# A transformer block on one core: gates ahead of the merges, operands made on demand, and a head that starts in 128-row pieces

## The chip, the cores and the metric

The kernel runs on one core of one Trainium2 chip. The metric is the device time of one execution, in microseconds (us). The core has five engines that run their own instruction streams: TensorE (PE, matrix products and transposes; PEld is its weight load), VectorE (DVE), ScalarE (ACT), GpSimd (POOL) and SyncE (SP). DMA transfers are issued from the queues of SP and ACT. They all run on the core's 16 DMA engines.

## The reference

One block of a hybrid network, in fp32, on x of 256 rows and 2048 columns (`T` = 256, `D` = 2048):

```python
h = rmsnorm(x, norm_ffn1);  x = x + 0.5 * (silu(h @ w1) * (h @ w3)) @ w2          # D_FF = 5632
h = rmsnorm(x, norm_mix)
(mq, mk, mv, mo, mi, mf, hq, hf, hi, hg, gate_m, gate_h) = split(h @ w_in)
y_m = mlstm_mixer(mq, mk, mv, mo, mi, mf, ...)       # 4 heads: conv, silu, gated attention, head norm
y_h = hgrn2_mixer(hq, hf, hi, hg, lb, ...)           # 8 heads: gated linear recurrence, head norm
merged = sigmoid(gate_m) * (y_m @ w_proj_m) + sigmoid(gate_h) * (y_h @ w_proj_h)
x = x + merged @ w_out
x = x + cross_attention(rmsnorm(x, norm_xattn), rmsnorm(mem, norm_mem), wq, wkv, wo)
h = rmsnorm(x, norm_ffn2);  x = x + 0.5 * (silu(h @ w1) * (h @ w3)) @ w2
return rmsnorm(x, norm_final)
```

All weights together are some 476 MB, and each is read once.

## The kernel before

**Products.** Every large product goes through `gemm_nat`. It makes a result of 256 x 512 (two PSUM banks from the pool `acc`, which has four) from 16 blocks of 128 rows of the weights, fewer for the projections. fp32 accuracy comes from a split: each operand is the sum of a high part rounded to fp32r and a low part, and three products are made per block: high by high (line 248), high by low weight (249), low operand by high weight (250). With two halves of the rows that is 6 products per block of 128 rows, 96 per full result of 2048 rows.

**Weights.** A `Unit` is a tile of 4 x 128 weight rows by 512 columns (1024 KB), loaded on SP's queue into one of four raw tiles (`wr`). A `Sub` is half of it: two blocks. `split` makes the high part (`wh`) with a cast on ACT and the low part (`wl`) with a subtraction on DVE, 1024 elements per partition each. `run` goes through the list of steps: before each Sub it loads units up to 7 Subs ahead, splits up to 3 ahead, then writes the 12 products and calls `tick`.

**Operands.** The left operand of a product is a pair of tiles (`oh`, `ol`) of 128 x 4 x 256, high and low, already transposed. A pair is turned either on PE (`turn`: four transposes of 128x128 per half, then cast and subtraction out of PSUM) or on DVE (`turn_on_vector`: 16 transposes of 32-row strips, `tt`, over four ticks, then cast and subtraction). These pairs and most other intermediate tiles come from one pool, `s4`, with 22 tiles.

**The planner.** Work beside the products is held in two lists. `timed` holds functions with the tick from which they are due (`after`). `bg` is a first-in, first-out list of background pieces: the HGRN and mLSTM mixers and the preparation of mem. `Paced` (line 90 is its call) adds up a planned cost per DVE and ACT instruction, a base plus a price per element. `tick` lets pieces go only while the planned backlog is under 2 us behind PE's planned time. `written` makes sure that a pair has been written before it is used, by running timed pieces; `flush` runs everything that is outstanding. Within each engine the instructions are put in order by the framework's scheduler, which may move an instruction ahead of an earlier one that has to wait.

**The mixer's end.** After the mLSTM values, for each of four column blocks c the kernel made the two gate products (gm, gh: 96 products each, from the norm's operands), then the projections of y_h (`evac_h`) and y_m (`evac_m`, which also adds and starts to turn the merged block). After the gates of c = 0 stood a flush, since the projections need `Y["h"]` and `Y["m"]`, which the background pieces make. Then four products with w_out follow.

**The head.** `setup` loads the identity, the first gains and, later, the other constants (705 KB) and small vectors on ACT's queue. `first` issues x in four chunks and the first weight units on SP's queue (`load_x`), turns x chunk 0 on PE, and puts the turns of the other chunks and the squares of the norm on ticks 1 to 7. The norm's factor is applied after the product, so the products wait only for x and the gains.

Of the kernel before, what the change touches and what calls it, by code (L numbers as in the profile page):

```python
# [19 lines left out]
P = 128  # L20
# [79 lines left out]
class Core:  # L100
    def __init__(self, nc):
        self.tensor, self.gpsimd, self.sync = nc.tensor, nc.gpsimd, nc.sync
        self.vector, self.scalar = Paced(nc.vector, 0.13, 0.00106), Paced(nc.scalar, 0.22, 0.00082)


class Block:
# [71 lines left out]
    def next_timed(self):  # L178
        i = min(range(len(self.timed)), key=lambda i: self.timed[i][0])
        self.timed.pop(i)[1]()  # L180

    def flush(self):
        while self.timed or self.bg:
            if self.timed:
                self.next_timed()
            else:
                self.bg.popleft()()

# [35 lines left out]

    def gemm_nat(self, ops, wap, n0, n, evac, kts=None, row0=0, late=0):

# [5 lines left out]
        def mm_for(k0, nk):  # L234
            def mm(hi, lo, ts=(0, 1)):
                if k0 == 0:
                    box["ps"] = [self.pacc([P, n]) for _ in range(2)]
                if k0 >= nkt - 2 * late and len(ts) == 2:
                    ts = (0,)
                    box.setdefault("late", []).append(lambda: mm(hi, lo, (1,)))  # L240
                for j in range(nk):
                    kt = k0 + j
                    xh, xl = self.written(pairs[kt // 4])
                    for t in ts:
                        sl = slice(t * P, (t + 1) * P)
                        a_h, a_l = xh[:, kt % 4, sl], xl[:, kt % 4, sl]
                        o = box["ps"][t]
                        nc.tensor.matmul(o, a_h, hi[:, j, :], start=(kt == 0), stop=False)  # L248
                        nc.tensor.matmul(o, a_h, lo[:, j, :], start=False, stop=False)  # L249
                        nc.tensor.matmul(o, a_l, hi[:, j, :], start=False, stop=(kt == nkt - 1))  # L250
# [16 lines left out]

    def turn(self, src, gain, dst, halves=(0, 1)):

        nc = self.nc  # L270
        hi, lo = dst
        for h in halves:
            ps = self.ps([P, 2, T])
            for j in range(2):
                for t in range(2):
                    c = (2 * h + j) * P
                    nc.tensor.transpose(ps[:, j, t * P:(t + 1) * P], src(t)[:, c:c + P], self.ident)  # L277
            if gain is None:
                nc.scalar.copy(hi[:, 2 * h:2 * h + 2, :], ps)
                nc.vector.tensor_sub(lo[:, 2 * h:2 * h + 2, :], ps, hi[:, 2 * h:2 * h + 2, :].bitcast(F32))  # L280
            else:
                for j in range(2):
                    k = 2 * h + j
                    g = gain[:, k:k + 1]
                    nc.scalar.activation(hi[:, k, :], ps[:, j, :], AF.Copy, scale=g)
                    nc.vector.scalar_tensor_tensor(
                        lo[:, k, :], in0=ps[:, j, :], scalar=g, in1=hi[:, k, :].bitcast(F32),
                        op0=ALU.mult, op1=ALU.subtract)
            if h == 1:
                self.unwritten.pop(id(dst), None)  # L290

    def pair(self):
# [3 lines left out]

    def written(self, p):

        while id(p) in self.unwritten:
            self.next_timed()  # L300
        return p

# [43 lines left out]
    def setup(self):  # L346
# [20 lines left out]

        def load(group):
            st = self.const.tile([P, P], F32, name=self.nm("stage"))
            first = group[0][1]  # L370
            for name, o, n in group:
                src = a[name]
                dims = " ".join("abc"[:len(src.shape)])
                src = src.rearrange(f"{dims} -> ({dims})")
                nc.scalar.dma_start(st[o - first:o - first + n, :], src.rearrange("(k p) -> k p", p=P))
            end = group[-1][1] + group[-1][2]
# [6 lines left out]
            return turn  # L383

        nc.scalar.dma_start(self.ident, a["consts"][:, :P])
        turn_first = load(groups[0])
        nc.vector.memset(self.mhalf, -0.5)

        def rest():
            nc.scalar.dma_start(c[:, P:], a["consts"][:, P:])  # L390
            turns = [load(g) for g in groups[1:]]
            self.gbias = self.const.tile([P, 8], F32, name="gbias")
            nc.scalar.dma_start(self.gbias[:, 0:4], a["mlstm_ig_bias"][0].partition_broadcast(P))
            nc.scalar.dma_start(self.gbias[:, 4:8], a["mlstm_fg_bias"][0].partition_broadcast(P))

# [6 lines left out]
        self.after(12, rest)  # L402
        return turn_first

    def lower_bounds(self):
# [36 lines left out]
    def rstd_of(self, ss, n, dim):  # L442
# [7 lines left out]
    def squares(self, src, ss_col):  # L450
        junk = self.t2([P, 512], name="junk")
        self.nc.scalar.activation(junk[:, :src.shape[-1]], src, AF.Square, accum_out=ss_col)

# [20 lines left out]

    def squares_of(self, n, c):
        for t in range(2):
            self.squares(self.x[c][:, t, :], n.ss[:, t, c:c + 1])
        n.count += 1
# [16 lines left out]
    def ffn(self, norm, w1, w3, w2, chunk_done, end=False):  # L495
        nc = self.nc
        ops = LazyOps(lambda: norm().ops)
        for f0, f1 in ((0, 6), (6, 11)):
            us = [None] * (f1 - f0)
            for f in range(f0, f1):  # L500
# [15 lines left out]

                self.gemm_nat(ops, w1, f * 512, 512, evac_a)
                self.gemm_nat(ops, w3, f * 512, 512, evac_b)
# [11 lines left out]
    def mixer(self, norm, chunk_done):  # L530
# [82 lines left out]

        merged = [None] * 4
        G = {}
        for c in range(4):
            for key, base in (("gm", 7176), ("gh", 9224)):
                def evac_g(ps, key=key):
                    r = norm().rstd
                    G[key] = self.t4([P, 2, 512], name=key)  # L620
                    for t in range(2):
                        nc.scalar.activation(G[key][:, t, :], ps[t], AF.Sigmoid, scale=r[:, t:t + 1])
                self.gemm_nat(ops, w, base + 512 * c, 512, evac_g)
            if c == 0:
                self.do(lambda: self.flush())

            def evac_h(ps):
                for t in range(2):
                    nc.vector.tensor_mul(G["gh"][:, t, :], ps[t], G["gh"][:, t, :])

            def evac_m(ps, c=c):
                gm, gh = G["gm"], G["gh"]
                for t in range(2):
# [15 lines left out]
    def hgrn_levels(self, h, b):  # L649
# [149 lines left out]
    def mlstm_weights(self, m):  # L799
# [17 lines left out]
        def head(h):  # L817
# [258 lines left out]
    def build(self):  # L1076
# [9 lines left out]

        def first(turn_gains):
            self.load_x()
            n = begin("norm_ffn1")
            n.ops = [self.pair() for _ in range(4)]  # L1090
            src = lambda c: (lambda t: self.x[c][:, t, :])
            turn_gains()
            for i in range(8):
                c, h = i // 2, i % 2
                fn = lambda c=c, h=h: self.turn(src(c), n.gain[:, 4 * c:4 * c + 4], n.ops[c], (h,))
                if i < 2:
                    fn()
                else:
# [78 lines left out]
```

## Time and profile before

| | |
|---|---|
| median of 3 runs | 2555.0 us (2554.29 to 2555.2) |
| the profiled execution | 2555.04 us |
| its span, first to last instruction | 2553.2 us |
| granted TensorE clock, mean | 0.998 |
| ACT table loads | 34, 43.6 us |
| DMA | 479.92 MB, mean 188 GB/s |

Times in the views are microseconds from the start of the span. A row of the timeline is start, duration, engine, line, operation, output <- input, count, and in brackets the idle time of the engine before it and what ended it. A row of waits is: who waited, for whom, us in total, times, longest. A row of windows gives the stretch, its length, busy time and number of instructions of PE, PEld, DVE, ACT and POOL, then granted clock, DMA share and GB/s. A row of groups gives count, busy us, mean ns, and the idle time before them. Products overlap in PE, so the length of one in a row (0.39) is more than the distance from one to the next.

### The profile page before, as it was taken

The page shows a single profiled execution, that of the slowest core. Times are in us where ns is not written, and L with a number is a line of the kernel's source. Part 1 is how long each engine was busy: PE and PEld are TensorE (multiplying, and loading weights), DVE is VectorE, ACT ScalarE, POOL GpSimd, SP SyncE. Part 2 cuts the span into 40 slices and gives each one's busy share as a digit, 9 for nine tenths or more (in the row PEclk, how much of TensorE's full clock was granted, in tenths as well). Part 3 has the DMA queues.
Part 4 walks back from the last instruction along what each step waited for, and adds up shares of the span by engine and source line. Part 5 has one row for each costly group of instructions (what it writes and reads, how often), then busy time and mean ns, then how long its engine had stood idle before and what let it go on. Part 6 is the DMA issues. An engine that isn't in the chain of part 4 may idle for free.

```text
span 2553.2 us, 29044 instructions
## 1 busy us (share of the span) xinstructions
PE 2528.8 (99%) x11431; PEld 2104.7 (82%) x11431; DVE 1730.7 (68%) x2384; ACT 1201.8 (47%) x1385; POOL 13.5 (1%) x21
## 2 busy tenths in 40 slices
PE   8999999999999999999999999999999999999998
PEld 7888888888888898787888888888888888888887
DVE  5767644767768878967666787677767574457664
ACT  5444434444455565644444454444544443344443
POOL 0000000000000000000000000000000000000000
PEclk9999999999999999999999999999999999999999
DMA  7665565565555545545555565555566556555653
GB/s 262 197 193 189 195 198 190 189 198 190 193 190 185 176 138 165 183 163 181 190 191 197 187 212 180 170 175 173 190 198 190 191 196 197 188 192 194 214 189 128
DMA packets 243305, 479.92 MB, mean 188 GB/s; under 512 B 8008, under 2 KB 14432, under 8 KB 243168
## 3 DMA queue, kind: packets, MB, share of 16 engines
q1 hardware_dynamic: 242016, 476.15, 57.4%
q10 hardware_dynamic: 1152, 1.92, 0.2%
q8 instruction: 89, 1.46, 0.2%
q14 instruction: 48, 0.39, 0.0%
HBM read 475.94 MB, written 2.10 MB: 187 GB/s over the span
## 4 chain that ended last, share of the span: by engine, by line
PE 92%; DVE 6%; issue 1%; ACT 0%; DMA 0%; POOL 0%; SPq 0%; POOLq 0%; ACTq 0%
PE pa L250 30%; PE pa L248 30%; PE pa L249 30%; DVE wl L90 2%; DVE tt L90 2%; PE ps L726 1%; DVE ol L90 1%; DVE cv L90 0%; PE ps L277 0%; DMA x<-in_x 0%; PE ps L966 0%; PE ps L967 0%; PE ps L965 0%; POOL rstd L447 0%; ACT kn L90 0%
## 5 line engine op out<-in xcount | busy, mean ns | idle before, releaser
L90 DVE TENSOR_TENSOR wl<-wr,wh 128x1024 fp32r<-128x1024 f32 (+1 forms) x904 | 1094.2, 1213 | 721.6 <-ACT wh L90 715.0
L90 ACT CAST wh<-wr 128x1024 fp32r<-128x1024 f32 (+1 forms) x904 | 942.0, 1045 | 1141.9 <-PE pa L250 1091.3
L248 PE MATMUL pa<-wh,oh 128*128 128x512 f32 (+1 forms) x3616 | 1409.7, 390 | 7.0 <-ACT oh L90 4.4
L249 PE MATMUL pa<-wl,oh 128*128 128x512 f32 (+1 forms) x3616 | 1403.6, 388 | 2.3 <-DVE wl L90 2.3
L250 PE MATMUL pa<-wh,ol 128*128 128x512 f32 (+1 forms) x3616 | 1402.5, 388 | 0.2 <-DVE ol L90 0.2
L248 PEld LDWEIGHTS pa<-wh,oh 128*128 128x128 f32 x3616 | 680.0, 188 | 143.3 <-ACT oh L90 4.8
L249 PEld LDWEIGHTS pa<-wl,oh 128*128 128x128 f32 x3616 | 680.2, 188 | 141.1 <-DVE wl L90 5.5
L250 PEld LDWEIGHTS pa<-wh,ol 128*128 128x128 f32 x3616 | 679.7, 188 | 138.8 <-DVE ol L90 0.7
L90 DVE STREAM_TRANSPOSE tt<-sil 32x256 f32<-32x256 f32 x352 | 153.6, 436 | 6.8
L90 DVE STREAM_TRANSPOSE tt<-x 32x256 f32<-32x256 f32 x144 | 62.8, 436 | 2.8
L90 ACT CAST oh<-tt 128x1024 fp32r<-128x1024 f32 x29 | 30.6, 1054 | 39.7 <-DVE tt L90 39.7
L90 ACT ACT_TABLE_LOAD x34 | 43.6, 1283 | 10.1 <-DVE rs L90 3.1
L90 ACT ACTIVATE oh<-tt,cols 128x256 fp32r<-128x256 f32 x52 | 23.3, 500 | 47.7 <-DVE tt L90 47.7
L90 ACT ACTIVATE sil<-pa,rstd 128x512 f32<-128x512 f32 x44 | 29.8, 689 | 17.8 <-PE pa L250 17.7
L90 DVE TENSOR_TENSOR ol<-tt,oh 128x1024 fp32r<-128x1024 f32 x29 | 35.4, 1220 | 1.6 <-ACT oh L90 1.4
L90 DVE STREAM_TRANSPOSE tt<-kn 32x256 f32<-32x256 f32 x64 | 27.9, 436 | 5.6 <-ACT kn L90 4.5
L90 DVE SCALAR_TENSOR_TENSOR sil<-pa,rstd,sil 128x512 f32<-128x512 f32 x44 | 31.0, 743 | 0.0
L90 DVE STREAM_TRANSPOSE qt<-qn 32x256 f32<-32x256 f32 x64 | 27.9, 436 | 4.1 <-ACT qn L90 3.0
L90 ACT ACTIVATE oh<-ps,cols 128x256 fp32r<-128x256 f32 x44 | 20.3, 473 | 21.4 <-DVE ol L90 15.6
L90 DVE COPY_PREDICATED at<-cst,ps 128x128 f32<-128x128 int32 x80 | 22.8, 328 | 10.6 <-PE ps L726 10.0
L90 ACT ACTIVATE junk<-x 128x512 f32<-128x512 f32 x40 | 24.9, 625 | 7.6 <-DVE x L90 7.0
L90 DVE SCALAR_TENSOR_TENSOR ol<-ps,cols,oh 128x256 fp32r<-128x256 f32 x44 | 20.7, 480 | 10.8 <-ACT oh L90 10.5
(174 smaller groups left out, 649.4 us busy)
## 6 DMA issues: line engine op xcount, KB each, us to landing
wr<-in_ffn_w SPq DMA_DIRECT2D x263, 1024.0 KB, 5.2
wr<-in_w_in SPq DMA_DIRECT2D x80, 1024.0 KB, 5.1
wr<-in_xattn_wkv SPq DMA_DIRECT2D x32, 1024.0 KB, 5.4
wr<-in_w_out SPq DMA_DIRECT2D x16, 1024.0 KB, 5.1
wr<-in_xattn_wq SPq DMA_DIRECT2D x16, 1024.0 KB, 5.0
wr<-in_xattn_wo SPq DMA_DIRECT2D x16, 1024.0 KB, 5.1
wr<-in_w_in SPq DMA_DIRECT2D x12, 688.0 KB, 4.1
wr<-in_w_proj_h SPq DMA_DIRECT2D x8, 1024.0 KB, 5.0
```

Source lines behind the costliest of these rows:

```text
L90: return fn(out, *args, **kw)
L248: nc.tensor.matmul(o, a_h, hi[:, j, :], start=(kt == 0), stop=False)
L249: nc.tensor.matmul(o, a_h, lo[:, j, :], start=False, stop=False)
L250: nc.tensor.matmul(o, a_l, hi[:, j, :], start=False, stop=(kt == nkt - 1))
L726: nc.tensor.matmul(ps[:, i, :], kt[:, g, j * P:(j + 1) * P], S["qc"][:, 2 * g + j, :], start=True, stop=True)
```

## The change

Six things are changed.

1. **Planner costs.** DVE from 0.13 + 0.00106 per element to 0.19 + 0.00104, ACT from 0.22 + 0.00082 to 0.25 + 0.00085; each `rstd_of` adds 0.9 to DVE's planned end.
2. **Operands on demand.** `written` takes the list and the index, and runs timed and background pieces until the operand exists and is written. The flush in the mixer is gone.
3. **Gates first.** The gates of c = 0, 1, 2 come before merge(0), the gates of c = 3 after it, then merges 1 to 3.
4. **From DVE to ACT.** `prep_f` of HGRN, and `di` and the copies into r0 and r1 of the mLSTM weights.
5. **The head.** Products of zeros (`warm`), 9 before x is turned and 4 behind the first piece; the first unit's Subs are four of one block each (`fine`); x chunk 0 is turned in four pieces of 128 columns, each followed by the split of its Sub; other turns and squares get other ticks; a first activation on the zeros.
6. **Order and queues.** The turns, the squares and the splits of the first 8 ticks are kept in program order on their engines. The constants and small vectors that are loaded at tick 12 are issued on SP's queue instead of ACT's.

```diff
-        self.vector, self.scalar = Paced(nc.vector, 0.13, 0.00106), Paced(nc.scalar, 0.22, 0.00082)
+        self.vector, self.scalar = Paced(nc.vector, 0.19, 0.00104), Paced(nc.scalar, 0.25, 0.00085)
...
+    def next_piece(self):
+        if self.timed:
+            self.next_timed()
+        else:
+            self.bg.popleft()()
...
-        self.nc.scalar.copy(s.hi, raw)
-        self.nc.vector.tensor_sub(s.lo, raw, s.hi.bitcast(F32))
+        pin = self.tc.keep_in_program_order if self.now < 8 else lambda ins: ins
+        pin(self.nc.scalar.copy(s.hi, raw))
+        pin(self.nc.vector.tensor_sub(s.lo, raw, s.hi.bitcast(F32)))
...
-                    xh, xl = self.written(pairs[kt // 4])
+                    xh, xl = self.written(pairs, kt // 4)
...
-            u = Unit(wap, row0 + k0 * P, 4, n0, n, 2)
-            for q in range(2):
-                self.steps.append(Sub(u, q, mm_for(k0 + 2 * q, 2)))
+            ns = 4 if fine and k0 == 0 else 2
+            u = Unit(wap, row0 + k0 * P, 4, n0, n, ns)
+            for q in range(ns):
+                self.steps.append(Sub(u, q, mm_for(k0 + 4 // ns * q, 4 // ns)))
...
+    def turn_piece(self, src, gain, dst, k, pin):
+        nc = self.nc
+        hi, lo = dst
+        ps = self.ps([P, T])
+        for t in range(2):
+            pin(nc.tensor.transpose(ps[:, t * P:(t + 1) * P], src(t)[:, k * P:(k + 1) * P], self.ident))
+        g = gain[:, k:k + 1]
+        pin(nc.scalar.activation(hi[:, k, :], ps, AF.Copy, scale=g))
+        pin(nc.vector.scalar_tensor_tensor(lo[:, k, :], in0=ps, scalar=g, in1=hi[:, k, :].bitcast(F32),
+                                           op0=ALU.mult, op1=ALU.subtract))
+        if k == 3:
+            self.unwritten.pop(id(dst), None)
...
-    def written(self, p):
-        while id(p) in self.unwritten:
-            self.next_timed()
-        return p
+    def written(self, ops, i):
+        while ops[i] is None or id(ops[i]) in self.unwritten:
+            self.next_piece()
+        return ops[i]
...
+        self.warm_tile = self.t2([P, P], name="warm")
+        nc.vector.memset(self.warm_tile, 0.0)
         nc.scalar.dma_start(self.ident, a["consts"][:, :P])
-        turn_first = load(groups[0])
+        turn_first = load(groups[0], nc.scalar)
+        self.tc.keep_in_program_order(
+            nc.scalar.activation(self.t2([P, 8], name="first"), self.warm_tile[:, 0:8], AF.Square))
...
-            nc.scalar.dma_start(c[:, P:], a["consts"][:, P:])
-            turns = [load(g) for g in groups[1:]]
+            nc.sync.dma_start(c[:, P:], a["consts"][:, P:])
+            turns = [load(g, nc.sync) for g in groups[1:]]
...
+    def warm(self, n):
+        ps = self.ps([P, P])
+        for _ in range(n):
+            self.nc.tensor.matmul(ps, self.warm_tile, self.warm_tile, start=True, stop=True)
...
         nc.gpsimd.tensor_tensor(r, ms, self.mhalf[:, :n], op=ALU.pow)
+        nc.vector.end += 0.9
...
-            if c == 0:
-                self.do(lambda: self.flush())
...
+        for c in range(3):
+            gates(c)
+        merge(0)
+        gates(3)
+        for c in range(1, 4):
+            merge(c)
...
-                nc.vector.tensor_scalar(f[:, i, :], f[:, i, :], self.oml[:, hd:hd + 1], self.lb[:, hd:hd + 1],
-                                        op0=ALU.mult, op1=ALU.add)
+                nc.scalar.activation(f[:, i, :], f[:, i, :], AF.Identity, scale=self.oml[:, hd:hd + 1],
+                                     bias=self.lb[:, hd:hd + 1])
...
-                nc.vector.tensor_scalar(di, self.ident, ig[t], None, op0=ALU.mult)
+                nc.scalar.activation(di, self.ident, AF.Copy, scale=ig[t])
...
-            nc.vector.tensor_copy(r0[:, 128:129], lf[0])
-            nc.vector.tensor_copy(r1[:, 0:129], lf[1].broadcast_to([P, 129]))
+            nc.scalar.copy(r0[:, 128:129], lf[0])
+            nc.scalar.copy(r1[:, 0:129], lf[1].broadcast_to([P, 129]))
...
         def first(turn_gains):
+            self.warm(9)
             self.load_x()
             n = begin("norm_ffn1")
             n.ops = [self.pair() for _ in range(4)]
             src = lambda c: (lambda t: self.x[c][:, t, :])
+            pin = self.tc.keep_in_program_order
             turn_gains()
-            for i in range(8):
+            first_subs = [st for st in self.steps if isinstance(st, Sub)][:4]
+            for k in range(4):
+                self.turn_piece(src(0), n.gain, n.ops[0], k, pin)
+                if k == 0:
+                    self.warm(4)
+                self.split(first_subs[k])
+            for i in range(2, 8):
                 c, h = i // 2, i % 2
-                fn = lambda c=c, h=h: self.turn(src(c), n.gain[:, 4 * c:4 * c + 4], n.ops[c], (h,))
-                if i < 2:
-                    fn()
-                else:
-                    self.after(i - 1, fn)
+                fn = lambda c=c, h=h: self.turn(src(c), n.gain[:, 4 * c:4 * c + 4], n.ops[c], (h,), pin)
+                self.after((1, 2, 4, 5, 6, 7)[i - 2], fn)
             for c in range(4):
-                self.after(4 + c, lambda c=c: self.squares_of(n, c))
+                self.after((5, 6, 8, 9)[c], lambda c=c: self.squares_of(n, c, pin=pin))
```

More of the change, by code (lines that the diff above doesn't have):

```diff
@@ L223, in run, with gemm_nat @@
         self.flush()
-    def gemm_nat(self, ops, wap, n0, n, evac, kts=None, row0=0, late=0):
+    def gemm_nat(self, ops, wap, n0, n, evac, kts=None, row0=0, late=0, fine=False):
         nc = self.nc
@@ L266, in gemm_nat, with turn @@
         self.do(finish)
-    def turn(self, src, gain, dst, halves=(0, 1)):
+    def turn(self, src, gain, dst, halves=(0, 1), pin=lambda ins: ins):
         nc = self.nc
@@ L366, in setup, with load @@
         self.stages = []
-        def load(group):
+        def load(group, engine):
             st = self.const.tile([P, P], F32, name=self.nm("stage"))
@@ L374, in load @@
                 src = src.rearrange(f"{dims} -> ({dims})")
-                nc.scalar.dma_start(st[o - first:o - first + n, :], src.rearrange("(k p) -> k p", p=P))
+                engine.dma_start(st[o - first:o - first + n, :], src.rearrange("(k p) -> k p", p=P))
             end = group[-1][1] + group[-1][2]
@@ L515, in evac_b @@
                     self.turn_on_vector(s, None, us[f - f0])
-                self.gemm_nat(ops, w1, f * 512, 512, evac_a)
+                self.gemm_nat(ops, w1, f * 512, 512, evac_a, fine=f == 0 and not end)
                 self.gemm_nat(ops, w3, f * 512, 512, evac_b)
@@ L611, in mixer, with gates @@
         self.do(lambda: self.bg.extend(self.mlstm_out(M, MV, MO)))
-        merged = [None] * 4
-        G = {}
-        for c in range(4):
+        merged, G = [None] * 4, {}
+        def gates(c):
             for key, base in (("gm", 7176), ("gh", 9224)):
@@ L619, in evac_g, with merge, evac_m @@
                     r = norm().rstd
[L620 removed]
+                    g = G[key, c] = self.t4([P, 2, 512], name=key)
                     for t in range(2):
[L622 removed]
+                        nc.scalar.activation(g[:, t, :], ps[t], AF.Sigmoid, scale=r[:, t:t + 1])
                 self.gemm_nat(ops, w, base + 512 * c, 512, evac_g)
[L624 to L625 removed]
+        def merge(c):
             def evac_h(ps):
                 for t in range(2):
[L629 to L632 removed]
+                    nc.vector.tensor_mul(G["gh", c][:, t, :], ps[t], G["gh", c][:, t, :])
+            def evac_m(ps):
+                gm, gh = G["gm", c], G["gh", c]
                 for t in range(2):
```

25 lines of the change are left out of this document (11 added, 14 removed).

## The prediction

> **What bounds the kernel now.** I read the page first: busy shares, then the chain that ended last.
>
> ```profile
> PE 2528.8 (99%) x11431; PEld 2104.7 (82%) x11431; DVE 1730.7 (68%) x2384; ACT 1201.8 (47%) x1385; POOL 13.5 (1%) x21
> PE 92%; DVE 6%; issue 1%; ACT 0%; DMA 0%; POOL 0%; SPq 0%; POOLq 0%; ACTq 0%
> ```
>
> TensorE (PE) is busy for 2528.8 of 2553.2 us, so 24.4 us of idle time is nearly all there is to win, unless products run slower than they could. The second view lists PE's waits.
>
> ```profile
> PE ps L381 <- DMA stage<-in_norm_ffn: 4.8, 1, 4.8
> PE pa L248 <- ACT oh L90: 4.4, 1, 4.4
> PE pa L248 <- ACT wh L90: 2.6, 1, 2.6
> PE pa L249 <- DVE wl L90: 2.3, 5, 0.5
> ```
>
> Four places: two at the start, one long wait for an operand (oh), and five short waits for the low part of a weight split. The third view counts PE's instructions (the x behind PE busy) by stretch; the row of 200 to 250 us is the steady state.
>
> ```profile
> 10.00:19.53 9.53, 9.11 (x32) 6.89 (x33) 5.88 (x7) 6.54 (x14) 0.00 (x0) 1.00 1.05 386
> 200.00:250.00 50.00, 50.00 (x222) 41.42 (x221) 35.15 (x45) 22.23 (x23) 0.00 (x0) 1.00 0.58 190
> 1020.00:1030.00 10.00, 8.50 (x36) 6.37 (x36) 9.65 (x19) 3.26 (x4) 0.00 (x0) 1.00 0.43 136
> 1030.00:1040.00 10.00, 9.22 (x39) 6.94 (x38) 9.82 (x20) 5.62 (x9) 0.00 (x0) 1.00 0.52 181
> 1040.00:1050.00 10.00, 10.00 (x44) 7.98 (x43) 9.71 (x18) 4.21 (x4) 0.00 (x0) 1.00 0.66 210
> 1147.89:1159.70 11.81, 7.15 (x16) 4.79 (x16) 11.30 (x19) 3.48 (x6) 0.00 (x0) 0.71 0.16 46
> ```
>
> Steady state is 50/222 = 0.225 us per product. Three stretches fall short. 1147.89 to 1159.70 holds 16 products, worth 3.6 us, in 11.81: **8.2 us lost**, of which only 4.4 are the wait. 1020 to 1040 holds 75 where 88 fit: 13 x 0.225 = **2.9 us lost**, with VectorE (DVE) busy 9.65 and 9.82 of 10. And 10.00 to 19.53 holds 24 products and 8 transposes. The chain gives four transposes at full pace:
>
> ```profile
> 15.31 0.43 PE pa L248
> ...
> 18.89 0.23 PE pa L249
> 19.12 0.23 PE pa L250
> 19.35 0.44 PE ps L277 x4
> ```
>
> So that stretch is worth 24 x 0.225 + 8 x 0.11 = 6.3 us and takes 9.53: **3.2 us lost**, because products there start every 0.43 us until about 16.1 and every 0.23 after that.
>
> **The change, part by part.**
>
> *Gates first (mixer).* The timeline around the loss:
>
> ```profile
> 1129.75 1.37 ACT L90 ACTIVATE gh<-pa,rstd 128x512 f32<-128x512 f32 x2 [1.17 <-PE pa L250]
> ...
> 1144.71 7.18 DVE L90 STREAM_TRANSPOSE tt<-mo 32x256 f32<-32x256 f32 x16
> ...
> 1147.67 0.39 PE L250 MATMUL pa<-wh,ol 128*128 128x512 f32 x1
> 1152.48 0.68 PE L248 MATMUL pa<-wh,oh 128*128 128x512 f32 x1 [4.42 <-ACT oh L90]
> ```
>
> After the first two gate products flush() writes out everything outstanding. PE gets halfway through proj_m, and the second mLSTM operand is still being turned on DVE (the 16 transposes of mo) until 1151.9. PE stops for 4.4 us. Then products start 0.43 us apart, at a granted clock of one half:
>
> ```profile
> 1154.50:1159.00 4.50, 4.50 (x11) 3.48 (x11) 4.50 (x7) 0.20 (x2) 0.00 (x0) 0.50 0.18 29
> ```
>
> The change puts four more gate products (gm, gh of c = 1, 2) ahead of merge(0): 4 x 96 x 0.225 = 86 us of PE work whose operands (the norm's) have long been there. PE would want that operand at 1147.9 + 86 = 1234, and the chain that makes it ended at 1152. Even if the planner, whose costs rise, stretches the remaining 70 us of background work by a fifth, some 65 us of cover are left. I take the whole **8.2 us**; bounds 0 (an equally long wait somewhere else) and 8.2. Total PE work is unchanged: the same products in another order.
>
> *Planner costs and work moved from DVE to ScalarE (ACT).* In 1020 to 1040 the wait is always DVE's subtraction wl. The planner releases background work while it believes that DVE is under 2 us behind. It counts a DVE operation of 256 elements at 0.13 + 256 x 0.00106 = 0.40 us; the trace has 0.436, and 0.478 for others. So DVE is really further behind than planned.
>
> ```profile
> L90 DVE STREAM_TRANSPOSE tt<-g 32x256 f32<-32x256 f32 x32 | 14.0, 436 | 0.6
> L90 DVE SCALAR_TENSOR_TENSOR ol<-tt,cols,oh 128x256 fp32r<-128x256 f32 x8 | 3.4, 478 | 0.0
> L90 DVE TENSOR_SCALAR di<-cst,gs 128x128 f32<-128x128 f32 x8 | 2.3, 282 | 0.1
> L90 DVE COPY r<-lf 128x129 f32<-128x129 f32 x4 | 0.9, 222 | 0.0
> ```
>
> The new costs give 0.19 + 256 x 0.00104 = 0.456, about the mean of the two. The gate weights' di and r (2.3 + 0.9 us of DVE, plus four one-column copies at 0.15) go to ACT, and so do prep_f's eight operations of 0.41. ACT is busy 3.26 and 5.62 of 10 in those rows, so 0.3 to 0.5 us each are hidden there; if ACT were full, the casts wh would be late, and each late cast stalls PE as a late wl does. I take **2.6 of the 2.9 us**; bounds 0 (the pacing only moves the crowding) and 3.2 (the smaller waits of 1050 to 1070 go too).
>
> *The head.* The timeline of the first 15 us:
>
> ```profile
> 1.65 0.44 ACTq L390 DMA_DIRECT2D cst<-in_consts  x1
> 4.84 0.25 PE L381 MATMUL ps<-cst,stage 16*128 16x16 f32 x1 [4.84 <-DMA stage<-in_norm_ffn]
> 5.03 2.37 PE L277 MATMUL ps<-cst,x 128*128 128x128 f32 x8
> 8.90 1.04 ACT L90 CAST wh<-wr 128x1024 fp32r<-128x1024 f32 x1 [0.99 <-DMA wr<-in_ffn_w]
> 9.98 1.23 DVE L90 TENSOR_TENSOR wl<-wr,wh 128x1024 fp32r<-128x1024 f32 x1 [1.55 <-ACT wh L90]
> 10.00 1.22 PE L248 MATMUL pa<-wh,oh 128*128 128x512 f32 x2 [2.60 <-ACT wh L90]
> 11.63 0.69 PE L277 MATMUL ps<-cst,x 128*128 128x128 f32 x2 [0.42 <-DMA x<-in_x]
> ```
>
> Before, the first product waits for a cast of 1024 elements that begins when half the first weight tile lands (8.90). Then PE meets transposes of the second x chunk, which lands at 11.6, ahead of the products already possible.
>
> (a) *Pieces.* The first cast has 512 elements. Between 0.47 us (256 elements) and 1.04 (1024) a line gives 0.66, so 0.4 us earlier. The subtraction shrinks alike, 1.22 to about 0.68 (the 128x512 additions of this trace).
>
> ```profile
> L90 ACT ACTIVATE oh<-ps,cols 128x256 fp32r<-128x256 f32 x16 | 7.3, 473 | 7.1 <-PE ps L277 5.8 <-DVE ol L90 1.3
> L90 DVE TENSOR_TENSOR gm<-gm,gh 128x512 f32<-128x512 f32 x6 | 3.8, 683 | 0.0
> ```
>
> In the kept order DVE then needs 0.48 + 0.68 = 1.16 us per piece, and PE 6 x 0.225 = 1.35: PE is the slower of the two, after one wait of about 0.5 for the first low part.
>
> (b) *The constants leave the head.* The 705 KB issued at 1.65 on ACT's queue shared the DMA engines with x and the first weights. In the first 9 us:
>
> ```profile
> q1 hardware_dynamic: 771, 1.48, 53.3%
> q10 hardware_dynamic: 320, 0.80, 25.6%
> ```
>
> q10, ACT's queue, moved 0.80 of 2.28 MB. Now the constants are issued on SP behind the x chunks and first weights. 0.72 MB at the 386 GB/s of the row 10.00:19.53 are up to 1.85 us; I take 1.3, since only what went ahead of the first half tile counts (bounds 0 and 1.85). Eleven more small loads join SP's queue; behind them stand weight loads, for which four raw tiles are a cover of some 10 us. I take nothing, bound 2 us lost.
>
> (c) *Products of zeros.* 13 fp32 products of 128 columns. Four of that kind take 0.88 us at full clock, and the second row follows the first by 0.22:
>
> ```profile
> 1050.96 0.38 PE L831 MATMUL ps<-r,cst 128*128 128x129 f32 x2
> 1051.18 0.39 PE L832 MATMUL ps<-r,cst 128*128 128x129 f32 x2
> ```
>
> Nine cost 2.0 us at full and 4 at half clock, from about 1.2 us on (an estimate: one memset behind DVE's first instruction at 0.8): over near 5, when PE got its first input anyway (4.84). The four behind the first two transposes cost 0.9 to 1.7 and end before 8.3. They hide behind the DMA wait; without that cover they would cost those 0.9 to 1.7. What they should buy is full pace at the first product: twelve products at 0.43 instead of 0.225 are 2.4 of the 3.2 us lost. The column of the granted clock reads 1.00 in the head, so I go by the distance of the products.
>
> The Trainium skill (TensorE: Matmul & The Clock Gate, Part 1) says that some 3.4 us of activity open the clock. Here the trace is slower: products began at 1152.48, the clock was still a half until 1159.00 and products came 0.23 us apart from 1159.5, seven us later, so by the row zeros from 1.2 us would open it near 8.2, just in time. The same page's Part 4 says that transposes do not count as busy for it, which speaks against this part and gives the first rival below.
>
> Sum of the head: the first product at 8.3 instead of 10.00 (1.7 us) and a loss of 0.9 (first low part, second x chunk) instead of 3.2 (2.3 us): **4.0 us**. Bounds: start 9.6, clock slow until about 13.5 (0.4 + 0.7 = 1.1), and start 7.8 with 0.5 lost (2.2 + 2.7 = 4.9).
>
> *Merges in a row.* Before, gates stood between the merges. Now merge(1) to merge(3) follow each other. DVE per merge, from the rows:
>
> ```profile
> L90 DVE TENSOR_TENSOR wl<-wr,wh 128x1024 fp32r<-128x1024 f32 x73 | 89.3, 1225 | 71.5 <-ACT wh L90 71.0
> L90 DVE STREAM_TRANSPOSE tt<-gm 32x256 f32<-32x256 f32 x48 | 20.9, 435 | 0.8
> ```
>
> 8 x 1.225 + 16 x 0.435 + 6 x 0.683 + 1.22 (the merged low part) = 22.1 us, against PE's 96 x 0.225 = 21.6. Two of the three are turned on DVE: 2 x 0.5 = 1.0 us too much, about half of which the planner can push into w_out's products. I take **0.5 us lost**; bounds 0 and the loss rate of 1020 to 1040 (2.9 us in 20) over 43 us, 6.2.
>
> Sum: 8.2 + 2.6 + 4.0 - 0.5 = 14.3 us off the profiled execution's 2555.04 us (span 2553.2 and 1.84 around it): **2540.7 us**. The median of the runs shown, 2555.0, is the same to 0.04.
>
> **The rivals.**
>
> 1. *Clock and DMA gain fail in the head.* The transposes let the clock fall, or the first weights land no earlier: head 1.1 instead of 4.0, **2543.6**. For it: slow products after a stop in two places of the trace. Against: PE now works from 1.2 us on. Chance 0.2.
> 2. *DVE becomes the bound of the merges*, 22.1 against 21.6, at the rate of 1020 to 1040: 5.7 more than I took, **2546.4**. Against: the planner's costs rise exactly for such a stretch. Chance 0.14.
> 3. *The change does not do what it says*: the long wait stays, at merge(0): **2548.9**. Against: 82 us of cover. Chance 0.05.
> 4. *Slower: the pool of 22 operand tiles runs full.* At merge(0) the norm's operands hold 8, Y 8, the three pairs of gates 6: all 22. merged[0] needs three more (tt, oh, ol), the next gates two. If their evacuation stalls, both accumulator pairs fill and PE stops until norm operands come free in gh3. Price: 8.2 us for each stop of the kind seen at 1147. From three such stops on (24.6 against 14.3 + 5.1) the kernel is slower; four, one for each of gates(3) and merges 1 to 3: **2573**. Against: before, c = 3 wanted 23 tiles (8 + 8 + 6 merged + gm), and the page's waits show no PE stop there. Chance 0.04.
> 5. *Several of 1 to 3 at once*: about **2549 to 2552**, chance 0.07.
>
> **How the numbers follow.** The forecast keeps 0.5. The low end, 2537.5, is all upper bounds (4.9 + 3.2 + 8.2 = 16.3, hence 2538.7) and a us for the small waits elsewhere. The high end, 2549, takes in rivals 1 to 3 and leaves out 4 and most of 5. A measurement of this kernel tells 0.2% from no change, 5.1 us: faster means below 2549.9. Faster holds the forecast, rivals 1 to 3 and a little less: 0.88; same, most of 5: 0.07; slower, 4 and an unseen rest: 0.05.
>
> **What would show it.** Head: the first weight product near 8.3 and products 0.23 us apart from the start; the first weight cast near 7.6. Wrong: 0.43 distances up to 13 us. Mixer: no PE wait for oh over 1 us between 1080 and 1250, and no 50 us row with a granted clock under 1.00. Stretch 1000 to 1070: waits for wl below 0.5 us in sum. New waits for wl or for a free tile within merges 1 to 3 would show rival 2 or 4. The prediction is wrong if the span falls by less than 6 us although the wait of 1152 is gone.

## The result and the profile after

| | before | after |
|---|---|---|
| median | 2554.64 us (6 runs, 2553.87 to 2555.2) | 2537.82 us (6 runs, 2537.64 to 2538.14) |
| ratio after to before, 95% interval | | 0.9934 (0.9922 to 0.9947) |
| span of the profiled execution | 2553.2 us | 2535.9 us |

The kernel is 16.8 us (0.66%) faster; 14.3 were forecast (2540.7), and the range 2537.5 to 2549.0 holds the result near its low end. The page of the changed kernel, busy shares and chain:

```profile
PE 2525.7 (100%) x11457; PEld 2105.7 (83%) x11457; DVE 1727.5 (68%) x2363; ACT 1209.7 (48%) x1413; POOL 14.4 (1%) x21
PE 98%; ACT 0%; DVE 0%; issue 0%; DMA 0%; SPq 0%; ACTq 0%; POOLq 0%; POOL 0%
```

PE's share of the chain rose from 92 to 98%, DVE's 6% are gone. PE's busy time hardly fell (2528.8 to 2525.7, with the products of zeros now in it): what went is time between products, and products at half pace. PE's waits, all of them:

```profile
PE ps L432 <- DVE mhalf L90: 1.1, 1, 1.1
PE pa L253 <- DVE wl L90: 0.2, 1, 0.2
```

Line 432 is the first product of zeros, waiting for its memset. The 4.4 us for an operand is gone, and the five waits of 0.5 for wl as well. The windows that fell short before now hold as many PE instructions as fit (the x behind PE busy):

```profile
1020.00:1030.00 10.00, 10.00 (x45) 8.28 (x45) 9.68 (x19) 5.28 (x6) 0.00 (x0) 1.00 0.33 108
1030.00:1040.00 10.00, 10.00 (x45) 8.26 (x44) 9.64 (x18) 3.64 (x4) 0.00 (x0) 1.00 0.44 133
1147.89:1159.70 11.81, 11.81 (x56) 9.80 (x55) 7.13 (x20) 5.42 (x13) 0.69 (x1) 1.00 0.50 172
```

DVE is nearly as full at 1020 to 1040 as before (9.68 and 9.64 of 10, against 9.65 and 9.82), yet PE no longer waits for it. The head, from the timeline:

```profile
1.05 4.21 PE L432 MATMUL ps<-warm 128*128 128x128 f32 x18 [1.05 <-DVE mhalf L90]
5.41 0.78 PE L303 MATMUL ps<-cst,x 128*128 128x128 f32 x2
6.02 1.06 PE L432 MATMUL ps<-warm 128*128 128x128 f32 x8
7.19 0.62 ACT L90 CAST wh<-wr 128x512 fp32r<-128x512 f32 x1 [0.49 <-DMA wr<-in_ffn_w]
7.86 0.73 PE L252 MATMUL pa<-wh,oh 128*128 128x512 f32 x2
8.59 0.51 PE L253 MATMUL pa<-wl,oh 128*128 128x512 f32 x1
8.93 0.39 PE L254 MATMUL pa<-wh,ol 128*128 128x512 f32 x1
9.16 0.40 PE L253 MATMUL pa<-wl,oh 128*128 128x512 f32 x1
```

The weights land at 7.19 instead of 8.90, the first weight product starts at 7.86 instead of 10.00, and from 8.93 on products come 0.23 us apart.

**Where the 17.3 us of the span came from.** Both kernels make the same 10848 weight products, so the start of the n-th one can be compared. It is earlier by 2.1 us at the first, 4.9 at the 25th, 3.8 at the 1001st, 16.7 at the 5201st (behind the mixer) and 17.3 at the last. A second count takes the distance from each PE instruction to the next, less the median distance of instructions of its shape, and sums it over stretches of the span; this is called lost time below. Some 3 us in the third column come in every kernel from small fp32 products of 256 columns, and from the product behind each group of them, which are spaced unequally; they are no waits.

```
us lost            0-60   1000-1090   1090-1280   1500-1800
before              7.6       4.6        11.7         1.6
after               4.7       0.2         3.3         0.9
difference          2.9       4.4         8.4         0.7
```

In the first column 0.9 us more are gained than the sum shows: PE starts 3.8 us earlier (1.05 instead of 4.84), which the sum does not count, and the zeros themselves take 2.8 us at full pace, which it does not count either. The head gave 3.8 us, the crowded stretch 4.4, the mixer's end 8.4, cross-attention 0.7.

### The profile page after: what moved, and what is told of

Read it like the earlier page. It is cut to its first block, busy times and chain, and to the rows that moved or that the text cites. A ratio compares the mean times of both kernels' runs of the same rounds, so it can differ in the third digit from the quotient of the medians.

```text
span 2535.9 us, 29109 instructions
## 1 busy us (share of the span) xinstructions
PE 2525.7 (100%) x11457; PEld 2105.7 (83%) x11457; DVE 1727.5 (68%) x2363; ACT 1209.7 (48%) x1413; POOL 14.4 (1%) x21
## 4 chain that ended last, share of the span: by engine, by line
PE 98%; ACT 0%; DVE 0%; issue 0%; DMA 0%; SPq 0%; ACTq 0%; POOLq 0%; POOL 0%
PE pa L253 32%; PE pa L252 32%; PE pa L254 32%; PE ps L762 1%; PE ps L1002 0%; PE ps L1003 0%; PE ps L1001 0%; PE ps L282 0%; DVE wl L90 0%; ACT wh L90 0%; DMA wr<-in_ffn_w 0%; ACT junk L90 0%; PE ps L1076 0%; DVE ol L90 0%; ACT oh L90 0%
## 5 line engine op out<-in xcount | busy, mean ns | idle before, releaser
L90 DVE TENSOR_TENSOR wl<-wr,wh 128x1024 fp32r<-128x1024 f32 (+2 forms) x906 | 1093.9, 1211 | 701.6 <-ACT wh L90 694.0
L90 ACT CAST wh<-wr 128x1024 fp32r<-128x1024 f32 (+2 forms) x906 | 942.0, 1043 | 1121.7 <-PE pa L254 1075.4
L90 ACT ACTIVATE oh<-ps,cols 128x256 fp32r<-128x256 f32 x44 | 20.7, 472 | 26.1 <-DVE ol L90 22.1
L90 DVE SCALAR_TENSOR_TENSOR ol<-ps,cols,oh 128x256 fp32r<-128x256 f32 x44 | 21.1, 480 | 11.9 <-ACT oh L90 11.9
```

The lines of the kernel that those rows point to most:

```text
L90: return fn(out, *args, **kw)
```

## The experiments

All runs but one start from the changed kernel; their times are to be compared with its 2537.82 us. They were made on several chips, on which the kernel before took 2554.06 to 2554.74 us, so a difference of some 0.5 us in the whole time says little. The head moves from run to run as well: in the seven traces with the same first 15 us of work (the changed kernel, late_squares, old_costs, dve_f, old_both, two_gates, old_merge) the first weight product starts between 7.82 and 8.37 us and the 25th between 14.59 and 15.15. A price in the head that is read from one trace is good to half a microsecond.

**1. no_zeros.** Do the products of zeros buy the pace?

```diff
-            self.warm(9)
...
-                if k == 0:
-                    self.warm(4)
```

> The changed kernel (2537.8 us) without its 13 products of zeros. Theory (zeros buy the clock): the first weight product starts where it did, near 7.9 us, but products come 0.43 us apart instead of 0.23 until TensorE has worked for 4 to 7 us; 12 to 20 products at 0.2 more each are 2.4 to 4.0 us: 2540.2 to 2541.8. Rival (the transposes of x and the early start do it anyway): 2537.8, products 0.23 apart from the start.

Measured: 2539.3 us (2538.79 to 2539.63), span 2537.0. The timeline of PE:

```profile
6.03 1.75 PE L303 MATMUL ps<-cst,x 128*128 128x128 f32 x7 [0.46 <-DMA x<-in_x]
8.02 1.22 PE L252 MATMUL pa<-wh,oh 128*128 128x512 f32 x2 [0.25 <-ACT wh L90]
9.04 0.63 PE L253 MATMUL pa<-wl,oh 128*128 128x512 f32 x1
9.47 0.63 PE L254 MATMUL pa<-wh,ol 128*128 128x512 f32 x1
9.90 0.63 PE L253 MATMUL pa<-wl,oh 128*128 128x512 f32 x1
10.32 0.46 PE L254 MATMUL pa<-wh,ol 128*128 128x512 f32 x1
10.62 0.40 PE L252 MATMUL pa<-wh,oh 128*128 128x512 f32 x1
```

Without zeros the first products are 0.43 us apart, so the rival falls. But full pace comes at 10.6, after six products, not 12 to 20: the 25th product starts at 15.66 against 14.64. The zeros are worth 1.0 us there, 1.1 in the span and 1.5 by the medians, less than the theory's 2.4 to 4.0.

**2. consts_act.** Constants and small vectors back on ACT's queue.

```diff
-            nc.sync.dma_start(c[:, P:], a["consts"][:, P:])
+            nc.scalar.dma_start(c[:, P:], a["consts"][:, P:])
```

(the small vectors and gbias likewise)

> The changed kernel with the 705 KB of constants and the small vectors back on ACT's queue. Theory (the constants took DMA time from the first weights): they are issued near 1.7 us again, the first weight cast starts at 8.5 to 8.9 instead of 7.19, and the kernel takes 1.3 to 1.7 us more: 2539.1 to 2539.5. Rival (pieces and order alone made the head faster): cast within 0.3 us of 7.19 and 2537.8.

Measured: 2540.79 us (2539.98 to 2541.95), span 2538.3. ACT's timeline, and the DMA queues of SP (q1) and ACT (q10) in the first 9 us, in this run:

```profile
9.09 0.62 ACT L90 CAST wh<-wr 128x512 fp32r<-128x512 f32 x1 [2.19 <-DMA wr<-in_ffn_w]
```

```profile
q1 hardware_dynamic: 779, 1.49, 49.2%
q10 hardware_dynamic: 320, 0.80, 24.6%
```

The same view of the changed kernel:

```profile
q1 hardware_dynamic: 1169, 2.24, 72.0%
q10 hardware_dynamic: 176, 0.07, 5.0%
```

The first weights land 1.9 us later, and SP's queue moves 1.49 MB in 9 us where it moves 2.24 in the changed kernel. The theory holds; at the first product the price is the upper bound of the prediction (1.85; its 0.72 MB at 386 GB/s are 1.87), not the 1.3 that was taken. The whole time missed its 1.3 to 1.7: it is 3.0 us longer by the medians and 2.4 in the span. Half a microsecond of that is lost from 20 to 60 us (1.8 instead of 1.3); why was not tried.

**3. halves.** The first unit in two Subs, x chunk 0 in two halves.

```diff
-            for k in range(4):
-                self.turn_piece(src(0), n.gain, n.ops[0], k, pin)
+            for k in range(2):
+                self.turn(src(0), n.gain, n.ops[0], (k,), pin)
                 if k == 0:
                     self.warm(4)
                 self.split(first_subs[k])
```

(with `fine` off, the ticks of before, and the order of splits kept for the first 6 ticks instead of 8, since there are fewer Subs)

> The changed kernel with the first unit in two Subs of two blocks and x chunk 0 turned in two halves, order and zeros kept. Theory (pieces shorten the way to the first products): first product 0.4 us later than 7.86, first low part 0.5 later again, in all 0.9 us: 2538.7. Rival (what the pieces win is given back at products 36 to 192, where splits are late): 2537.8.

Measured: 2539.52 us (2539.32 to 2539.82), span 2537.6; the first product starts at 9.05:

```profile
9.05 0.73 PE L252 MATMUL pa<-wh,oh 128*128 128x512 f32 x2 [1.20 <-ACT wh L90]
10.31 0.50 PE L253 MATMUL pa<-wl,oh 128*128 128x512 f32 x1 [0.53 <-DVE wl L90]
```

and ACT ahead of it:

```profile
7.59 0.47 ACT L90 ACTIVATE oh<-ps,cols 128x256 fp32r<-128x256 f32 x1 [0.55 <-DVE ol L90]
7.96 1.04 ACT L90 CAST wh<-wr 128x1024 fp32r<-128x1024 f32 x1
```

The pieces are worth 1.7 us, twice the expectation: in the kept order the cast of 1024 elements also stands behind the second cast of x on ACT, which waits for DVE, and begins at 7.96 where the changed kernel's begins at 7.19. So the first product is 1.2 us late and not 0.4.

**4. no_order.** All three pins of the head off.

```diff
-        pin = self.tc.keep_in_program_order if self.now < 8 else lambda ins: ins
+        pin = lambda ins: ins
```

(and in `first`)

> The changed kernel without the kept order of turns, squares and splits. Theory (the order keeps the second x chunk's transposes behind the first products): TensorE meets transposes of chunk 1 before the products of the first pieces and waits for their data until some 10.8 us; 1 to 2 us more: 2538.8 to 2539.8. Rival (the scheduler finds the same order by itself): 2537.8.

Measured: 2537.28 us (2537.21 to 2537.34), span 2535.5. The rival holds, and more: PE's products follow in the same order at the start (first at 8.05, 25th at 14.82), and later this kernel is ahead. The windows from 20 to 40 us, the changed kernel's first, then no_order's:

```profile
20.00:40.00 20.00, 19.79 (x89) 15.42 (x88) 10.80 (x15) 16.03 (x33) 0.70 (x1) 1.00 0.78 274
```

```profile
20.00:40.00 20.00, 20.00 (x93) 16.53 (x92) 12.44 (x18) 14.07 (x21) 0.70 (x1) 1.00 0.86 297
```

Four more PE instructions fit. Without pins ACT makes its first squares at 15.56 us instead of 23.24. With pins it stands idle ahead of a turn for 1.3 to 1.5 us, five times from 14 to 32 us, and makes the squares afterwards, ahead of casts of weights.

**5. late_squares and first_order.** Two changes aimed at that microsecond: the squares put off, and the pins kept for the first four pieces alone.

```diff
-                self.after((5, 6, 8, 9)[c], lambda c=c: self.squares_of(n, c, pin=pin))
+                self.after((7, 8, 9, 9)[c], lambda c=c: self.squares_of(n, c, pin=pin))
```

> The changed kernel with the norm's squares put off from ticks 5, 6, 8, 9 to 7, 8, 9, 9. In its trace TensorE loses 0.9 us at 30 to 35 us, where the weight split waits for ACT behind two pairs of squares. Theory (ACT's squares are in the way of the casts): most of the 0.9 comes back, 2537.0. Rival (the pinned turns, each held 1.3 us by DVE, set the pace of ACT): 2537.8, or worse where four squares come together.

Measured: 2537.9 us (2537.7 to 2538.01), span 2536.1, and 1.2 us lost from 20 to 60 us instead of 1.3. The squares' place is not it.

```diff
-        pin = self.tc.keep_in_program_order if self.now < 8 else lambda ins: ins
+        pin = self.tc.keep_in_program_order if self.now < 1 else lambda ins: ins
...
-                fn = lambda c=c, h=h: self.turn(src(c), n.gain[:, 4 * c:4 * c + 4], n.ops[c], (h,), pin)
+                fn = lambda c=c, h=h: self.turn(src(c), n.gain[:, 4 * c:4 * c + 4], n.ops[c], (h,))
```

(and the squares free)

> The changed kernel with the order kept for the four pieces of x chunk 0 and their splits alone; later turns, squares and splits are free, as in no_order (2537.28 us), which reached product 24 at 14.82 us of its span instead of 14.64 but lost 0.2 us between 20 and 60 us instead of 1.3. Theory (the late pins, not the early ones, give back a microsecond): 1.0 us less than the changed kernel's 2537.82, some 2536.8 to 2537.2, the fastest of all. Rival (the early pins are what holds ACT up later, too): 2537.8.

Measured: 2537.39 us (2536.98 to 2538.72), span 2535.6; 0.2 us lost from 20 to 60. The late pins cost the microsecond, as the theory says; in the whole time only 0.4 us (first_order) and 0.5 us (no_order) are left of it, not the 1.0 of the theory. Part went where the first product starts 0.2 to 0.3 us later in these traces (8.17 and 8.05 against 7.86), part in cross-attention, where 0.3 us more are lost. That is a tenth of the 5.1 us that the prediction says a measurement tells from no change, so neither kernel is called faster than the changed one.

**6. old_costs, dve_f, old_both.** Which part cured the crowded stretch? The three edits: the planner's old costs, without the 0.9 (old_costs); prep_f back on DVE (dve_f); the old costs and prep_f, di and r on DVE (old_both).

```diff
-Paced(nc.vector, 0.19, 0.00104), Paced(nc.scalar, 0.25, 0.00085)
+Paced(nc.vector, 0.13, 0.00106), Paced(nc.scalar, 0.22, 0.00082)
```

```diff
-                nc.scalar.activation(f[:, i, :], f[:, i, :], AF.Identity, scale=self.oml[:, hd:hd + 1],
-                                     bias=self.lb[:, hd:hd + 1])
+                nc.vector.tensor_scalar(f[:, i, :], f[:, i, :], self.oml[:, hd:hd + 1], self.lb[:, hd:hd + 1],
+                                        op0=ALU.mult, op1=ALU.add)
```

> The changed kernel with the planner's old costs (and without the 0.9 after rstd_of); the moved work stays on ACT. Theory (costs too low let DVE fall behind): the waits for wl come back between 1000 and 1070 us; of the 4.5 us that TensorE lost there before, 2 to 4 return: 2539.8 to 2541.8. Rival (moving work to ACT did it): under 0.5 us lost there, 2537.8 to 2538.3.

> The changed kernel with prep_f's eight operations of 0.41 us back on DVE, new costs kept. Theory (the costs pace DVE whatever it holds): 2537.8, no wait for wl over 0.2 us between 750 and 1070. Rival (the moved work made the room): waits for wl of 0.5 us each return, 1 us or more.

> The changed kernel with old costs and with prep_f, di and r back on DVE. If costs and moved work together are the whole of the stretch 1000 to 1070: 4 to 5 us return there, 2541.8 to 2542.8. If the stretch was cured by something else (gates first shifts no work before 1080, so this would be a surprise): 2537.8. The difference to old_costs is what the moved work is worth under the old costs.

Measured: old_costs 2550.05 us (2548.98 to 2550.6), dve_f 2537.96 (2537.78 to 2539.3), old_both 2542.75 (2542.65 to 2543.22). By the count of lost time from 1000 to 1090 us: 11.9, 0.2 and 4.8 us, against 0.2 after and 4.6 before. old_both and dve_f came out as expected: together the parts are worth the whole of the stretch, and under the new costs the place of prep_f does not matter. old_costs was a miss by 8 us, and a surprise: with the old costs, moving work off DVE makes the stretch 7 us worse (11.9 against 4.8). Its PE waits, and the one that ACT had in the same stretch:

```profile
PE ps L869 <- DVE r L90: 2.1, 2, 1.7
PE pa L253 <- DVE wl L90: 2.1, 4, 0.9
PE ps L866 <- DVE r L90: 2.1, 1, 2.1
```

```profile
ACT di L90 <- DVE r L90: 12.7, 3, 6.1
```

In old_both PE's waits there are the known ones:

```profile
PE pa L253 <- DVE wl L90: 2.4, 6, 0.5
```

di, r0 and r1 have one tile each. On one engine, di and r follow each other. On two, ACT writes di, DVE makes r from it, and ACT cannot write the next di until then: each step waits in the queue of an engine that the old costs let run late, and PE stands at the fp32 products of r. Behind the wait at 1049 the granted clock is 0.50 from 1049.3 to 1056.1, which old_both does not have. This account of the queues is argued from the waits. With the new costs PE has no wait for r. So without the new costs the stretch is not cured, and prep_f's place does not matter with them; the moved work under the old costs is a danger. Two things were not run: di and r back on DVE under the new costs, and the new costs one by one (DVE's, ACT's, the 0.9).

**7. two_gates.** How much cover do the gates give?

```diff
-        for c in range(3):
+        for c in range(2):
             gates(c)
-        merge(0)
-        gates(3)
-        for c in range(1, 4):
+        for c in range(4):
             merge(c)
+            if c < 2:
+                gates(c + 2)
```

> The changed kernel with the gates of only two column blocks ahead of merge(0), 43 us less cover. In the changed kernel's trace the second mLSTM operand is complete at 1206.6 us and wanted near 1226. Theory A (the cover of 82 us that was forecast): the background work does not mind, 2537.8. Theory B (the new costs slowed the background work, and only 20 us of cover are left): merge(0) wants the operand 43 us earlier, near 1183, the pieces are forced out at once, and a stop of the old kind returns, 4 to 8 us: 2541.8 to 2545.8.

Measured: 2549.77 us (2549.28 to 2550.59), span 2547.5. Theory B holds, and the price is higher than its 8 us: 11.3 us more are lost from 1090 to 1280.

```profile
1191.04 7.18 DVE L90 STREAM_TRANSPOSE tt<-mo 32x256 f32<-32x256 f32 x16
...
1198.25 1.71 ACT L90 ACTIVATE oh<-tt,cols 128x256 fp32r<-128x256 f32 x4 [5.07 <-DVE tt L90]
1198.81 0.79 PE L252 MATMUL pa<-wh,oh 128*128 128x512 f32 x1 [6.26 <-ACT oh L90]
```

It is the picture of before, 46 us later: 16 transposes of mo in one go, PE stopped for 6.3 us, then products at half pace until 1201.8. In the changed kernel these transposes are spread between the splits and end with the operand's low part:

```profile
1202.05 1.79 DVE L90 STREAM_TRANSPOSE tt<-mo 32x256 f32<-32x256 f32 x4
1203.88 1.23 DVE L90 TENSOR_TENSOR wl<-wr,wh 128x1024 fp32r<-128x1024 f32 x1
1205.02 1.67 DVE L90 SCALAR_TENSOR_TENSOR ol<-tt,cols,oh 128x256 fp32r<-128x256 f32 x4
```

The operand is complete at 1206.7, and the second half of proj_m, 24 products behind the evacuation at 1221.0, begins near 1226. So 20 us of cover are left.

**8. old_merge and b_gates.** The old order in the changed kernel, and the new order alone in the kernel before.

```diff
-        for c in range(3):
-            gates(c)
-        merge(0)
-        gates(3)
-        for c in range(1, 4):
-            merge(c)
+        for c in range(4):
+            gates(c)
+            if c == 0:
+                self.do(lambda: self.flush())
+            merge(c)
```

> The changed kernel with the old order at the mixer's end: two gate products, flush, merge, for each column block. Theory (gates first is worth the wait and the slow clock behind it): a stop of 4 us or more before proj_m's second half, a granted clock under 1.00 behind it, 8 us in all or more, since the background work now runs later: 2545.8 to 2549. Rival (the new costs alone thin the crowd at the flush): 2537.8 to 2540.

Measured: 2549.54 us (2549.14 to 2550.66); 11.4 us more lost from 1090 to 1280. Its PE waits:

```profile
PE pa L252 <- ACT oh L90: 5.0, 2, 3.1
PE pa L253 <- DVE wl L90: 2.0, 2, 1.9
```

No stop is over 4 us, unlike the expectation, but there are three of 1.9 to 3.1, and behind two of them the granted clock is 0.50 for 3.4 us (from 1145.2 and from 1155.4). The new costs do not cure the flush; with them it costs 11.4 us instead of 8.4. That more work is outstanding when it comes would explain it; this was not counted.

> The kernel before (2554.6 us) with gates first and operands on demand alone; head, costs and DVE work as before. Theory (the parts add up): 8.0 us less, 2546.6, no clock drop at 1150 us, the waits for wl at 1020 to 1040 still there. Rival (the three parts depend on each other, the stretch's crowding moves into the merges): 2548 to 2552.

Measured: 2546.8 us (2546.34 to 2547.21) against 2554.2 of the kernel before on the same chip, 7.4 less. The loss from 1090 to 1280 is 3.2, that of 1000 to 1090 stays at 4.7:

```profile
PE ps L384 <- DMA stage<-in_norm_ffn: 4.8, 1, 4.8
PE pa L252 <- DVE wl L90: 2.3, 5, 0.5
PE pa L251 <- ACT wh L90: 2.1, 1, 2.1
```

The long wait for oh is missing, the rest of the list is much like that of before. The part stands by itself.

## Why the prediction was right, step by step

| term of the sum | forecast | measured |
|---|---|---|
| gates first | 8.2 | 8.4 (b_gates alone: 7.4 of the time) |
| planner costs and moved work | 2.6 (0 to 3.2) | 4.4 |
| head | 4.0 (1.1 to 4.9) | 3.8 |
| merges in a row | -0.5 | 0 |
| cross-attention | not in the sum | 0.7 |
| sum | 14.3 | 17.3 of the span, 16.8 of the time |

The measured gain is larger than the sum of all the upper bounds, 16.3 us: the crowded stretch gave more than its bound, and cross-attention was no term. The range held by a few tenths, thanks to the microsecond that its low end kept for small waits elsewhere; that much of it was luck.

- **Gates first.** Right in size and mechanism. One step in it failed: "some 65 us of cover are left". The new costs spread the background work, the operand came at 1206.7 instead of 1152, and 20 us were left. With one block of gates fewer the stop is back (two_gates). The size came out because 20 are as good as 65, and that was luck: the prediction gave the long wait a chance of only 0.05 because of a cover that had mostly gone.
- **The crowded stretch** was mis-sized. I counted the products missing from 1020 to 1040, 2.9 us, and bounded the rest with 3.2. The loss lay over 1000 to 1070: each of the four longest waits, 0.5 us in the view, costs 0.67 from product to product. The view counts idle time only from the end of the product before (0.39 us long), while the next one would have started 0.23 us after its start. The mechanism (costs too low) was right. The moved work, which the prediction counted into the gain, is not shown to give any: prep_f's place makes no difference under the new costs, and under the old ones the moved work makes it worse.
- **The head.** The sum was right, its parts were not. Taken out one at a time, the constants are worth 1.9 instead of 1.3, the pieces 1.7 instead of about 0.9, the zeros 1.0 instead of 2.4, each good to half a microsecond; such prices need not add up. What reached the 25th product, 4.9 us, was the upper bound; 1.1 were given back by product 1000, nearly all of it at the late pins, which the prediction took to cost nothing. The "seven us" from which the zeros were judged, taken from the stop at 1152, did not hold for the head: without zeros full pace came 2.6 us after the first weight product, and with them PE was at full pace at 6.02 us, the transposes and zeros then 0.11 us apart, not near 8.2.
- **Rivals.** Rival 1 (the head's gain fails) and rival 3 (the long wait stays) did not occur: the first cast is at 7.19, products are 0.23 us apart from 8.93 on, and PE's waits hold none for oh. Rival 2 (DVE the bound of the merges) did not occur either: 22.1 us of DVE work were set against 21.6 us of products for each merge, but DVE is busy 55 of the 70 us from 1270 to 1340, about three merges, and PE has no wait there:

```profile
1270.00:1340.00 70.00, 70.00 (x310) 57.99 (x309) 55.19 (x75) 30.59 (x30) 0.00 (x0) 1.00 0.59 190
```

- Rival 4 (the pool runs full) shows its beginning: merged[0]'s low part is written at 1259.3, 13 us after its high part, when the norm's operands begin to come free. Nobody waits for it yet.

```profile
1259.32 1.23 DVE L90 TENSOR_TENSOR ol<-tt,oh 128x1024 fp32r<-128x1024 f32 x1 [0.18 <-PE pa L253]
```

That a full pool causes this delay is argued from the count of tiles, not tried.
- **Cross-attention.** Four waits of 0.13 us idle, in the row of 1550 to 1750 before (199.46 of 200 us busy), are gone (200.00 after). With the old costs the loss there is back: 1.6 in old_costs, old_both and b_gates, against 0.9 to 1.5 in the runs with the new ones. So it seems to belong to the planner's costs, too, though the scatter is nearly as large as the effect. The prediction had no term for them beyond the mixer.

## What to carry to other kernels

A consumer moved behind independent work hides a producer chain only while the planner's pace leaves cover: after any change of pace, read when the operand is complete and when it is wanted, here 1206.7 and 1226. Costs of a software planner should be those of the trace; here an under-count of about a tenth went with 4.4 us of lost time, and moving work to an idle engine did not help but hurt as long as the pace was wrong. In a head that waits for its first DMA, take everything that is not needed yet off every queue: here 705 KB on the other queue put the first weights off by 1.9 us.

## What was not expected of the hardware

- A half pace from the start lasted only six products, from 8.02 to 10.6 us, without the zeros, and from 10.00 to about 16.1 before. In both PE made transposes first, from 5.0 or 5.1 on. In the kernel before PE stood idle from 7.4 to 10.00, without the zeros for 0.25 us. The granted clock of the windows reads 1.00 there, but the trace's record of the clock only begins later, and time without a record counts as 1.00; in the head the distance of products shows the pace. The record begins at 16.0 us in the kernel before, 15.8 in b_gates and 10.4 in no_zeros, where the distances change. In the eleven runs with zeros it begins between 4.0 and 7.3 us, each time ahead of the first weight product.
- The stretches of half clock around a stop were of the same lengths in different runs: 6.8 us in the kernel before (1152.6 to 1159.5), in two_gates (1195.3 to 1202.1) and in old_costs, 3.4 us twice in old_merge. In two_gates half of it fell into the stop itself, so full pace was back some 3 us after the restart at 1198.81, not seven.
- 705 KB on ACT's queue delayed 512 KB on SP's queue by 1.9 us (7.19 to 9.09), about the whole time that they take by themselves at the 386 GB/s of the row 10.00:19.53.
